# One step of Strassen's scheme in the two output projections of a decoder trunk

## The chip, the cores and the metric

The kernel runs on one core of a Trainium2 chip, as one launch. The metric is the device time of the launch in microseconds (us). The kernel before takes 1911.1 us (median of 3 runs, 1909.24 to 1915.82).

## The reference

The input x has 1024 tokens of width 1024. Two layers follow one another, each with a residual sum, and a shared key and value projection lies between them:

```python
x = x + gated_deltanet_mixer(rms_norm(x, a_norm), ...)   # layer A
k_band, v_band = shared_kv(x, kv_norm, w_kv, k_gain)
x = x + swa_sink_mixer(rms_norm(x, b_norm), ...)         # layer B
# both mixers end in the same way, o is (1024 tokens, 2048):
return o.reshape(B, T, 2048).astype(h.dtype) @ w_out     # w_out (2048, 1024)
```

In layer A, o is the output of a gated delta rule in 8 heads of width 256, normed and multiplied by silu(z). In layer B it is that of a windowed attention with 32 heads of 64, again times silu(z). All is float32. The change touches only the two products `o @ w_out` and the sums with the residual that follow.

## The kernel before, in words

Every large product is made in three matmuls: each factor is cut into a high and a low part (`hi`, `lo`), and hi·hi, hi·lo and lo·hi are accumulated in PSUM. The gated outputs are written to DRAM as transposed rows, `ogT` in layer A and `og2` in layer B (`og` in the rows), 16 blocks of 128 channels by 1024 tokens.

`weight` (L122) makes one weight tile of 128x1024: a DMA of 512 KB on SP's queue into one of two `wraw` buffers, the high part on POOL (L134; weights with a gain are multiplied on POOL, L136, and get theirs on ACT), the low part on DVE (L138). Of the first two tiles after `wcount` is set to 0 or 1 the low part is made on POOL. `take` hands out the next tile and starts as many as `depth` says: two ahead in A, one in B.

`og_load` (L853) loads a quarter of 512 tokens (4 of the 16 blocks) in two DMAs of 512 KB on ACT's queue, casts each half (L862, ACT) and subtracts (L863, DVE).

`out_proj` (L865) is called once per layer. It goes over two halves of the tokens, two column halves `cp` of 512, four quarters `k4` of the channels, two column blocks `b` of 256. For each (k4, b) it takes a weight tile [4, 256], and for 4 token blocks c and 4 channel blocks kk issues three matmuls of 256 moving columns: 2 x 2 x 4 x 2 x 4 x 4 x 3 = 1536 matmuls a projection, 32 weight tiles. Both column halves of one token half share the loaded og; the second half's is loaded during cp = 1. The residual rows `xo` (four tiles of 512 KB for each half, L882) are loaded at (k4, b) = (2, 0). At the end of each cp, four evictions (L893, DVE) add PSUM onto them, and 256 KB stores follow. In A, `finish` then norms the half and transposes it between the matmuls that come next.

Each engine works its instructions in program order, as a scheduler has laid them out ahead of time; an instruction whose input isn't there holds up all behind it on that engine, the DMA issues of that queue too.

Of the kernel before, what the change touches and what calls it, by code (L numbers as in the profile page):

```python
# [64 lines left out]
class Kernel:  # L65
# [56 lines left out]
    def weight(self, src, shape, gain=None):  # L122
# [110 lines left out]
    def layer_a(self):  # L233
        nc, tc, I = self.nc, self.tc, self.I
        with ExitStack() as ctx:
# [72 lines left out]
            for h in range(AH):  # L308
# [6 lines left out]
                if h + 1 == AH:  # L315
                    back += [self.head_z(i, None) for i in late]
                    self.first = self.og_tiles(self.dl0, "kq", "vt")
                    self.og_load(self.ogT, 0, 0, self.first, self.raws)
# [546 lines left out]
    def out_proj(self, og, resid, cur, tiles, raws, px, acc, dst, finish):  # L865
# [3 lines left out]
        for half in range(2):  # L869
            xs, nxt = [], []  # L870
            for cp in range(2):
                cs = slice(cp * 512, cp * 512 + 512)
                ps = [acc.tile([P, 2, 256], F32, name="acc") for _ in range(4)]
                for k4 in range(4):
                    oh, ol = cur[k4]
                    for b in range(2):
                        hi, lo = self.take()
                        if cp == 0 and (k4, b) == (2, 0):
                            self.flush()
                            for c in range(4):  # L880
                                xs.append(px.tile([P, D], F32, name="xo", bufs=4))
                                nc.sync.dma_start(xs[c], resid[half * 4 + c])  # L882
                        for c in range(4):
                            ts = slice(c * P, c * P + P)
                            po = ps[c][:, b, :]
                            for kk in range(4):
                                nc.tensor.matmul(po, oh[:, kk, ts], hi[:, kk, :], start=(k4 + kk + b == 0), stop=False)  # L887
                                nc.tensor.matmul(po, oh[:, kk, ts], lo[:, kk, :], start=False, stop=False)  # L888
                                nc.tensor.matmul(po, ol[:, kk, ts], hi[:, kk, :], start=False, stop=(k4 + kk + b == 7))  # L889
                                if kk % 2:  # L890
                                    self.tick()
                            if (k4, b) == (3, 1):
                                nc.vector.tensor_tensor(out=xs[c][:, cs], in0=ps[c].rearrange("p b c -> p (b c)"),  # L893
                                                        in1=xs[c][:, cs], op=ALU.add)
                                nc.sync.dma_start(dst[half * 4 + c][:, cs], xs[c][:, cs])
                    if half == 0 and cp == 1:
                        nxt.append(tiles(k4))
                        self.og_load(og, 1, k4, nxt[-1], raws)
            cur = nxt
            finish(half, xs)  # L900
# [97 lines left out]
    def layer_b(self, last):  # L998
# [20 lines left out]
        def ahead():  # L1019
            for k4 in range(3):  # L1020
                self.og_load(self.og2, 0, k4, last[k4], raws)
# [4 lines left out]
        self.og_load(self.og2, 0, 3, last[3], raws)  # L1026
# [198 lines left out]
    def run(self):  # L1225
        nc, tc, I = self.nc, self.tc, self.I
        with ExitStack() as ctx:
# [11 lines left out]
            self.wpools, self.wcount = [self.wsp], 0  # L1239
            self.late = (6,)  # L1240
# [5 lines left out]
            with ExitStack() as c1:  # L1246
                hp = pool(c1, "hT")
                self.hT = self.hT_tiles(hp)
                with ExitStack() as c2:
# [23 lines left out]
                    def tiles(k4):  # L1273
                        return self.og_tiles(po, f"oh{k4}", f"ol{k4}") if k4 else self.og_tiles(self.dl0, "kq", "vt")

# [94 lines left out]
```

## Time and profile before

| | us |
|---|---|
| median of 3 runs | 1911.1 |
| profiled execution, its own time | 1906.83 |
| span of the profiled execution | 1905.1 |
| projection A, first to last matmul start | 911.41 to 1098.48 |
| projection B, first to last matmul start | 1716.71 to 1901.01 |
| PE busy in the whole span | 1828.6 (96%) |
| DVE, ACT, POOL busy | 1229.2, 807.5, 536.5 |

Times in the rows are us from the start of the span unless marked ns. PE is TensorE's matmul, PEld its weight load, DVE is VectorE, ACT ScalarE, POOL GpSimd, SP SyncE; a q behind an engine is its queue, which issues DMAs. The mean granted clock is 0.994 of full speed. Everything outside the two projections, some 1530 us, is the same code before and after, except for a few loads at their beginning.

### The profile page before, as it was taken

What the parts mean: (1) busy time and instruction counts of PE and PEld (TensorE: products, weight loads), DVE (VectorE), ACT (ScalarE), POOL (GpSimd) and SP (SyncE); (2) the same over time, 40 slices, a digit from 0 to 9 for tenths busy, and PEclk for the clock granted to TensorE, in tenths of its full rate; (3) what the DMA queues carried; (4) which work ended last, traced back from release to release, by engine and by line L of the source; (5) the groups of instructions that cost most, each with busy time, mean ns of one, the idle gap of its engine ahead of it and who ended that gap; (6) DMA issues with size and microseconds to landing.
All of it is one profiled execution on the core that took longest, in us unless ns stands there. A gap on an engine that the chain in (4) does not pass through costs nothing.

```text
span 1905.1 us, 33635 instructions
## 1 busy us (share of the span) xinstructions
PE 1828.6 (96%) x13186; PEld 1562.9 (82%) x13186; DVE 1229.2 (65%) x2860; ACT 807.5 (42%) x1939; POOL 536.5 (28%) x554
## 2 busy tenths in 40 slices
PE   5999999999999999989999999999999999999999
PEld 4677778787877777767999998888788788879999
DVE  6767776858596776775545266777776776753432
ACT  4545353534435252433112043557756666771100
POOL 2222332323222222221311232333433343322111
PEclk9999999999999999999999999999999999999999
DMA  4511111112011211121655321111201111225542
GB/s 148 122 56 34 56 45 53 37 34 67 23 57 34 65 36 56 45 67 51 238 165 168 111 89 45 40 35 51 67 29 51 56 40 51 73 72 194 190 168 81
DMA packets 150115, 147.62 MB, mean 77 GB/s; under 512 B 7114, under 2 KB 124356, under 8 KB 149956
## 3 DMA queue, kind: packets, MB, share of 16 engines
q1 hardware_dynamic: 139616, 128.30, 21.4%
q10 hardware_dynamic: 10340, 17.16, 2.9%
q8 instruction: 104, 1.70, 0.4%
q14 instruction: 55, 0.45, 0.1%
HBM read 115.00 MB, written 30.44 MB: 76 GB/s over the span
## 4 chain that ended last, share of the span: by engine, by line
PE 36%; DVE 8%; ACT 3%; POOL 3%; issue 2%; DMA 1%; POOLq 0%; SPq 0%; ACTq 0%; DVEq 0%
PE acc L887 6%; PE acc L889 6%; PE acc L888 6%; PE mm L939 3%; PE mm L940 3%; PE mm L941 3%; PE pv L1181 2%; ACT lsb L1150 1%; PE mm L165 1%; PE mm L163 1%; PE mm L161 1%; DVE lsb L1140 1%; DVE wlo L138 1%; POOL lsb L1154 1%; PE tp L1160 1%
## 5 line engine op out<-in xcount | busy, mean ns | idle before, releaser
L161 PE MATMUL mm<-hh,whi 128*128 128x512 f32 (+1 forms) x1040 | 427.1, 411 | 1.8 <-ACT hh L223 1.7
L163 PE MATMUL mm<-hl,whi 128*128 128x512 f32 (+1 forms) x1040 | 417.5, 401 | 1.0 <-DVE hl L224 0.7
L165 PE MATMUL mm<-hh,wlo 128*128 128x512 f32 (+1 forms) x1040 | 414.8, 399 | 0.0
L138 DVE TENSOR_TENSOR wlo<-wraw,whi 128x1024 fp32r<-128x1024 f32 x141 | 178.7, 1268 | 241.0 <-POOL whi L134 216.0
L134 POOL TENSOR_SCALAR whi<-wraw 128x1024 fp32r<-128x1024 f32 x112 | 122.8, 1097 | 476.3 <-PE acc L889 241.4
L161 PEld LDWEIGHTS mm<-hh,whi 128*128 128x128 f32 x1040 | 197.0, 189 | 36.9 <-issue 5.2
L165 PEld LDWEIGHTS mm<-hh,wlo 128*128 128x128 f32 x1040 | 196.7, 189 | 36.5 <-issue 4.2
L163 PEld LDWEIGHTS mm<-hl,whi 128*128 128x128 f32 x1040 | 197.2, 190 | 34.1 <-issue 4.2
L939 PE MATMUL mm<-whi,hh 128*128 128x256 f32 x608 | 180.5, 297 | 0.0
L463 DVE SCALAR_TENSOR_TENSOR acc<-u,cw,acc 128x512 f32<-128x512 f32 x192 | 162.7, 849 | 26.5 <-POOL acc L460 24.3
L940 PE MATMUL mm<-wlo,hh 128*128 128x256 f32 x608 | 172.2, 283 | 0.0
L941 PE MATMUL mm<-whi,hl 128*128 128x256 f32 x608 | 172.2, 283 | 0.0
L887 PE MATMUL acc<-whi,hh 128*128 128x256 f32 x512 | 145.0, 283 | 0.0
L889 PE MATMUL acc<-whi,hl 128*128 128x256 f32 x512 | 144.9, 283 | 0.0
L888 PE MATMUL acc<-wlo,hh 128*128 128x256 f32 x512 | 144.9, 283 | 0.0
L1150 ACT ACTIVATE lsb<-lsb,nm 128x128 f32<-128x128 f32 x256 | 99.8, 392 | 64.1 <-DVE se L1146 54.6
L939 PEld LDWEIGHTS mm<-whi,hh 128*128 128x128 f32 x608 | 116.0, 191 | 11.0 <-issue 10.8
L940 PEld LDWEIGHTS mm<-wlo,hh 128*128 128x128 f32 x608 | 116.3, 191 | 0.2
L941 PEld LDWEIGHTS mm<-whi,hl 128*128 128x128 f32 x608 | 116.0, 191 | 0.0
L460 POOL TENSOR_SCALAR acc<-u,cw 128x512 f32<-128x512 f32 x64 | 63.9, 998 | 183.8 <-ACT u L456 169.6
L1154 POOL TENSOR_TENSOR lsb<-lsb,den 128x512 f32<-128x512 f32 x64 | 68.5, 1070 | 152.6 <-DVE den L1153 51.9
L887 PE MATMUL acc<-whi,oh 128*128 128x256 f32 x384 | 108.5, 283 | 0.0
(351 smaller groups left out, 4287.2 us busy)
## 6 DMA issues: line engine op xcount, KB each, us to landing
wraw<-in_a_w_in SPq DMA_DIRECT2D x48, 512.0 KB, 3.9
wraw<-in_a_w_out SPq DMA_DIRECT2D x32, 512.0 KB, 3.9
wraw<-in_b_w_in SPq DMA_DIRECT2D x32, 512.0 KB, 4.0
wraw<-in_b_w_out SPq DMA_DIRECT2D x32, 512.0 KB, 4.1
og<-zs SPq DMA_DIRECT2D x32, 256.0 KB, 2.0
ogT<-zs SPq DMA_DIRECT2D x28, 256.0 KB, 2.1
btab<-lt SPq DMA_DIRECT2D x1, 4096.0 KB
dm<-gd SPq DMA_DIRECT2D x8, 512.0 KB, 3.7
```

The source lines that it names most:

```text
L134: nc.gpsimd.tensor_scalar(out=hi, in0=raw, scalar1=1.0, scalar2=1.0, op0=ALU.mult, op1=ALU.mult)
L138: (nc.gpsimd if self.wcount < 3 else nc.vector).tensor_tensor(out=lo, in0=raw, in1=self.f32(hi), op=ALU.subtract)
L161: nc.tensor.matmul(ps, hi[:, k, :], hh[:, k, :], start=(k == 0), stop=False)
L163: nc.tensor.matmul(ps, hi[:, k, :], hl[:, k, :], start=False, stop=False)
L165: nc.tensor.matmul(ps, lo[:, k, :], hh[:, k, :], start=False, stop=(k == KT - 1))
L463: nc.vector.scalar_tensor_tensor(out=acc, in0=u[:, t:t + 512], scalar=cw[:, t, blk:blk + 1], in1=acc, op0=ALU.mult, op1=ALU.add)
L887: nc.tensor.matmul(po, oh[:, kk, ts], hi[:, kk, :], start=(k4 + kk + b == 0), stop=False)
L888: nc.tensor.matmul(po, oh[:, kk, ts], lo[:, kk, :], start=False, stop=False)
L889: nc.tensor.matmul(po, ol[:, kk, ts], hi[:, kk, :], start=False, stop=(k4 + kk + b == 7))
L939: nc.tensor.matmul(ps, hh[:, k, ts], hi[:, k % 4, :], start=(k == 0), stop=False)
L940: nc.tensor.matmul(ps, hh[:, k, ts], lo[:, k % 4, :], start=False, stop=False)
L941: nc.tensor.matmul(ps, hl[:, k, ts], hi[:, k % 4, :], start=False, stop=(k == KT - 1))
```

## The change

The tokens, the 2048 channels and the 1024 columns are each cut in two. Instead of eight products of quadrants, seven are made (`PRODUCTS`), each from a sum or difference of og quadrants and of weight quadrants, with signs. Each product has 4 weight tiles j of [2, 512], 4 token blocks c, 2 channel blocks kk and three matmuls of 512 moving columns: 7 x 4 x 4 x 2 x 3 = 672 matmuls a projection.

```python
+    PRODUCTS = (
+        (((1, 0, 0),), ((1, 0, 1), (-1, 1, 1)), ((0, 1, 1), (1, 1, 1))),
+        (((1, 1, 0), (-1, 0, 0)), ((1, 0, 0), (1, 0, 1)), ((1, 1, 1),)),
+        ...
+    )   # terms of og (sign, t, k); terms of w (sign, k, c); sinks (t, q, sign)
...
         nc.sync.dma_start(raw, src)
+        if other is not None:
+            op, src2 = other
+            raw2 = view(self.raw2())
+            nc.sync.dma_start(raw2, src2)
+            nc.gpsimd.tensor_tensor(out=raw, in0=raw, in1=raw2, op=op)
...
-        if gain is None:
+        if other is not None:
+            nc.scalar.copy(out=hi, in_=raw)
+        elif gain is None:
...
+        def quadrant(t, k):
+            if (t, k) not in held:
+                r = held[t, k] = whole(place[t, k])
+                for i in (0, 4):
+                    nc.scalar.dma_start(r[:, i:i + 4, :], ogv[:, 8 * k + i:8 * k + i + 4, 512 * (1 - t):1024 - 512 * t])
...
+            src = [quadrant(t, k) for _, t, k in terms]
+            for j in range(2):
+                ...
+                    nc.vector.tensor_tensor(out=raw, in0=src[0][:, ks, :], in1=src[1][:, ks, :],
...
+                nc.scalar.copy(out=oh[:, js, :], in_=raw)
+                nc.vector.tensor_tensor(out=ol[:, js, :], in0=raw, in1=self.f32(oh[:, js, :]), op=ALU.subtract)
...
+                if (m, j) == (0, 3):
+                    self.flush()
+                    xs = [[px.tile([P, D], F32, name="xo", bufs=8) for _ in range(4)] for _ in range(2)]
+                    ...
+                            nc.sync.dma_start(xs[t][c], resid[(1 - t) * 4 + c])
...
+                        nc.tensor.matmul(ps[c], oh[:, k, ts], hi[:, kk, :], start=(j + kk == 0), stop=False)
...
+                        for t, q, sign in sinks:
+                            x = xs[t][c][:, 512 * q:512 * q + 512]
+                            if sign > 0:
+                                nc.vector.tensor_tensor(out=x, in0=ps[c], in1=x, op=ALU.add)
+                            else:
+                                nc.vector.tensor_tensor(out=x, in0=x, in1=ps[c], op=ALU.subtract)
```

Of a projection's 28 weight tiles 20 are sums or differences: two DMAs of 512 KB, the sum on POOL, the high part on ACT, the low part on DVE. The second raw tile lies in halves of `vv` in A (free once layer A's last gated rows are stored) and in a pool of its own in B. The og factors come as 14 half-products u, two for each product, in a ring of 3 places in A and 4 in B. u = 0 and 1 are loaded by `og_load`. Those after come from whole quadrants of 2.1 MB ("rooms"), each in two DMAs of 1 MB on ACT's queue; A takes layer A's dead inputs `hT` for that (`hh`, `hl` in the rows), B a new pool. Ten of the twelve need 20 DVE sums of 128x1024 in all; each of the 12 needs two casts on ACT and two subtractions on DVE. Each product is evicted onto the residual rows that it belongs to, 12 places in all: 48 evictions of 128x512 a projection. All eight residual tiles (4.2 MB) are loaded in product 0.

The start of projection B on ACT. Before (L862 casts og, L861 loads it, L1089 is silu of the last z, L1183 copies the attention's output):

```order
L1089 ACTIVATE zs_18798<-zs_18798 128x512
L862 CAST hh0_82<-qr_18812 128x1024
L862 CAST hh1_84<-qr_18816 128x1024
L861 DMA qr_18820<-og2_58 128x2x512
L861 DMA qr_18842<-og2_58 128x2x512
L861 DMA qr_18846<-og2_58 128x2x512
L862 CAST hh1_84<-qr_18820 128x1024
L862 CAST hh1_84<-qr_18842 128x1024
L862 CAST hh1_84<-qr_18846 128x1024
```

After (L926 casts og, L908 loads rooms, L141 casts weights; whi_18147 is the high part of the third weight tile, w2, and whi_18191 that of w3):

```order
L908 DMA room1_18092<-og2_58 128x4x512 x2
L908 DMA room0_18095<-og2_58 128x4x512 x2
L926 CAST hh1_84<-oraw_18098 128x1024
L926 CAST hh1_84<-oraw_18102 128x1024
L141 CAST whi_18147<-wraw_18142 128x1024
L908 DMA room2_18175<-og2_58 128x4x512
L926 CAST hh1_84<-oraw_18106 128x1024
L926 CAST hh1_84<-oraw_18110 128x1024
L908 DMA room2_18175<-og2_58 128x4x512
L926 CAST hh0_82<-oraw_18178 128x1024
L926 CAST hh0_82<-oraw_18182 128x1024
L141 CAST whi_18191<-wraw_18186 128x1024
```

The high parts of w2 and w3 stand on ACT now, behind casts of sums of rooms.

The start of projection A on ACT. Before (L841 is the last silu of A):

```order
L841 ACTIVATE acc_9324<-mm_9299 128x512
L862 CAST oh1_9391<-kt_9393 128x1024
L862 CAST oh1_9391<-dm_9397 128x1024
L861 DMA kt_9403<-ogT_57 128x2x512
L861 DMA dm_9407<-ogT_57 128x2x512
L862 CAST oh2_9401<-kt_9403 128x1024
L862 CAST oh2_9401<-dm_9407 128x1024
L861 DMA kt_9413<-ogT_57 128x2x512
L861 DMA dm_9417<-ogT_57 128x2x512
```

After (whi_9426 and whi_9434 belong to w1 and w2):

```order
L850 ACTIVATE acc_9327<-mm_9302 128x512
L908 DMA hh1_84<-ogT_57 128x4x512
L871 CAST oh0_9394<-kt_9398 128x1024
L871 CAST oh0_9394<-dm_9402 128x1024
L908 DMA hl1_85<-ogT_57 128x4x512
L926 CAST oh1_9396<-kt_9410 128x1024
L926 CAST oh1_9396<-dm_9414 128x1024
L908 DMA hl1_85<-ogT_57 128x4x512
L141 CAST whi_9426<-wraw_9422 128x1024
L141 CAST whi_9434<-wraw_9430 128x1024
```

Here also the high parts of w1 and w2 stand behind the casts of u = 1 and u = 2.

The start of projection A on SP. Before (L821 and L846 write the last gated rows of A, L130 loads weights, L882 residual rows):

```order
L821 DMA ogT_57<-zs_8743 128x512
L821 DMA ogT_57<-zs_8981 128x512
L846 DMA ogT_57<-acc_9324 128x512
L130 DMA wraw_9485<-in_a_w_out 128x4x256
L882 DMA xo_9653<-in_x 128x1024
L130 DMA wraw_9539<-in_a_w_out 128x4x256
L882 DMA xo_9655<-in_x 128x1024
L130 DMA wraw_9593<-in_a_w_out 128x4x256
L882 DMA xo_9657<-in_x 128x1024
```

After (L942 loads residual rows, L136 the second raw tile of a sum, L132 the first):

```order
L830 DMA ogT_57<-zs_8981 128x512
L855 DMA ogT_57<-acc_9327 128x512
L942 DMA xo_9542<-in_x 128x1024
L136 DMA vv_9374<-in_a_w_out 128x2x512 x2
L942 DMA xo_9543<-in_x 128x1024
L136 DMA vv_9374<-in_a_w_out 128x2x512 x2
L942 DMA xo_9544<-in_x 128x1024
L132 DMA wraw_9462<-in_a_w_out 128x2x512
L132 DMA wraw_9502<-in_a_w_out 128x2x512
L942 DMA xo_9545<-in_x 128x1024
L136 DMA vv_9374<-in_a_w_out 128x2x512
```

The second raw tiles of w1 and w2 (`vv`) stand behind the last write of gated rows; the first raw tiles were loaded earlier.

## Rows read from the trace of the kernel before

**Rows 1.** Timeline of PE: first and last matmul of each projection; start, length (us).

```profile
911.41 0.36 PE L887 MATMUL acc<-whi,kq 128*128 128x256 f32 x1
...
1098.48 0.28 PE L889 MATMUL acc<-whi,ol 128*128 128x256 f32 x1
...
1716.71 0.39 PE L887 MATMUL acc<-whi,hh 128*128 128x256 f32 x1
...
1901.01 0.28 PE L889 MATMUL acc<-whi,hl 128*128 128x256 f32 x1
```

**Rows 2.** Waits of PE from 905 to 1100 us; none from 1700 to 1905.

```profile
PE acc L888 <- POOL wlo L138: 1.2, 1, 1.2
```

**Rows 3.** Busy time by windows (us, count), granted clock, DMA share, GB/s.

```profile
930.00:1000.00 70.00, 70.00 (x593) 70.00 (x592) 27.57 (x25) 8.10 (x8) 14.60 (x13) 1.00 0.55 176
1750.00:1800.00 50.00, 50.00 (x419) 50.00 (x419) 20.47 (x18) 5.99 (x6) 9.44 (x9) 1.00 0.48 156
```

**Rows 4.** Timeline of PE: matmuls of 512 columns before projection A and in layer B.

```profile
903.23 0.39 PE L161 MATMUL mm<-hh,whi 128*128 128x512 f32 x1
...
905.95 0.39 PE L161 MATMUL mm<-hh,whi 128*128 128x512 f32 x1
...
1670.81 0.39 PE L163 MATMUL mm<-hl,whi 128*128 128x512 f32 x1
...
1671.74 0.39 PE L165 MATMUL mm<-hh,wlo 128*128 128x512 f32 x1
```

**Rows 5.** Single operations by line: count, duration min/median/max in ns, first, last start.

```profile
L138 DVE TENSOR_TENSOR wlo<-wraw,whi x141: 1180/1225/2776, 55.8 to 1890.9; 128x1024 fp32r<-128x1024 f32 x141
...
L138 POOL TENSOR_TENSOR wlo<-wraw,whi x7: 2342/2399/3304, 13.1 to 1730.5; 128x1024 fp32r<-128x1024 f32 x7
...
L134 POOL TENSOR_SCALAR whi<-wraw x112: 1040/1047/2137, 10.2 to 1889.9; 128x1024 fp32r<-128x1024 f32 x112
...
L136 POOL TENSOR_TENSOR wraw<-wraw,gcolb x36: 1892/1897/2933, 1081.8 to 1634.8; 128x1024 f32<-128x1024 f32 x36
...
L893 DVE TENSOR_TENSOR xo<-acc,xo x32: 679/691/694, 955.2 to 1901.3; 128x512 f32<-128x512 f32 x32
...
L862 ACT CAST hh<-qr x8: 1031/1044/1051, 1706.4 to 1726.9; 128x1024 fp32r<-128x1024 f32 x8
...
L863 DVE TENSOR_TENSOR hl<-qr,hh x8: 1212/1226/1909, 1707.5 to 1728.3; 128x1024 fp32r<-128x1024 f32 x8
```

**Rows 6.** Timeline of POOL and DVE beside each other in projection A.

```profile
914.32 2.06 DVE L863 TENSOR_TENSOR ol<-kt,oh 128x1024 fp32r<-128x1024 f32 x1
916.30 3.38 DVE L863 TENSOR_TENSOR ol<-dm,oh 128x1024 fp32r<-128x1024 f32 x1
...
913.28 2.03 POOL L134 TENSOR_SCALAR whi<-wraw 128x1024 fp32r<-128x1024 f32 x1 [1.76 <-DVE acc L845]
915.39 3.21 POOL L138 TENSOR_TENSOR wlo<-wraw,whi 128x1024 fp32r<-128x1024 f32 x1
...
958.74 0.69 DVE L893 TENSOR_TENSOR xo<-acc,xo 128x512 f32<-128x512 f32 x1 [0.75 <-DMA wraw<-in_a_w_out]
...
958.78 1.05 POOL L134 TENSOR_SCALAR whi<-wraw 128x1024 fp32r<-128x1024 f32 x1 [4.72 <-PE acc L889]
```

**Rows 7.** Busy time by windows with DMA at its highest, start of projection A.

```profile
916.00:920.00 4.00, 2.77 (x24) 2.57 (x23) 3.68 (x2) 0.00 (x0) 4.00 (x2) 1.00 1.00 370
```

**Rows 8.** Timeline of ACT (one cast) and of SP's queue (last writes).

```profile
932.44 1.05 ACT L862 CAST oh<-kt 128x1024 fp32r<-128x1024 f32 x1 [4.95 <-DMA kt<-ogT]
...
913.29 0.32 SPq L846 DMA_DIRECT2D ogT<-acc  x1
...
1713.05 5.82 SPq L1092 DMA_DIRECT2D og<-zs  x3
```

**Rows 9.** Timeline of PE after a long idle time, start of the program.

```profile
19.23 0.93 PE L216 MATMUL tr<-cst,kq 128*128 128x128 f32 x2 [11.59 <-DVE kq L209]
...
22.26 0.41 PE L165 MATMUL mm<-hh,wlo 128*128 128x256 f32 x1
```

More of the change, by code (lines that the diff above doesn't have):

```diff
@@ L1 @@
+import itertools
 from contextlib import ExitStack
@@ L120, in rsqrt, with weight @@
         return y
-    def weight(self, src, shape, gain=None):
+    def weight(self, src, shape, gain=None, other=None):
         nc = self.nc
@@ L863, in og_load @@
             nc.vector.tensor_tensor(out=ol[:, js, :], in0=raw, in1=self.f32(oh[:, js, :]), op=ALU.subtract)
-    def out_proj(self, og, resid, cur, tiles, raws, px, acc, dst, finish):
-        nc = self.nc
[L869 to L882, printed above, removed]
-                        for c in range(4):
[L884 to L900, printed above, removed]
@@ L1019, in ahead @@
         def ahead():
-            for k4 in range(3):
-                self.og_load(self.og2, 0, k4, last[k4], raws)
+            for k4 in range(2):
+                self.og_load(self.og2, 1, k4, last[k4], raws)
                 yield 0.0
@@ L1025, in layer_b @@
         self.flush()
-        self.og_load(self.og2, 0, 3, last[3], raws)
     @staticmethod
@@ L1239, in run @@
             self.wpools, self.wcount = [self.wsp], 0
+            self.raw2 = raw2 = lambda: self.wraw.tile([P, 1024], F32, name="wraw")
             self.late = (6,)
@@ L1271, in finish @@
                             self.later((15, 10)[half] + (2, .8)[half] * j, f)
[L1273 to L1280 removed]
+                    ring = [self.first] + [self.og_tiles(po, f"oh{i}", f"ol{i}") for i in range(2)]
+                    room = [self.hT[0][0], self.hT[1][0], self.hT[1][1]]
+                    spare = itertools.cycle(self.vv[:, n:n + 4, :].rearrange("p n c -> p (n c)") for n in (0, 4))
+                    self.raw2 = lambda: next(spare)
+                    self.out_proj(self.ogT, xv, ring, 1, self.raws, lambda i: self.f32(room[i]), px, acc, x1d, finish)
+                    self.raw2 = raw2
                     wk = [self.take(False), self.take(False)]
@@ L1303, in run @@
                     px = pool(c2, "px2", 2)
-                    self.out_proj(self.og2, x1d, last, lambda k4: last[k4],
-                                  lambda j: px.tile([P, 2, 512], F32, name="oraw"), px, pool(c2, "acc2", 6, space=PSUM), ov,
-                                  lambda half, xs: None)
+                    wraw2 = pool(c2, "wraw2", 2)
+                    self.raw2 = lambda: wraw2.tile([P, 1024], F32, name="wraw2")
+                    room = pool(c2, "room")
+                    self.out_proj(self.og2, x1d, last, 2, lambda j: px.tile([P, 2, 512], F32, name="oraw"),
+                                  lambda i: room.tile([P, KT, 512], F32, name=f"room{i}"), px,
+                                  pool(c2, "acc2", 6, space=PSUM), ov, lambda half, xs: None)
     def weights(self):
@@ L1325, in weights @@
                     yield col(self.win, b, None)
-        for _ in range(2):
-            for c in (0, 2):
-                for k in range(4):
-                    for b in range(2):
-                        yield four(rows("a_w_out"), k, c + b, None)
+        yield from self.product_weights(rows("a_w_out"))
         wkv = I["w_kv"].rearrange("(k p) c -> p k c", p=P)
@@ L1340, in weights @@
                 yield col(bin_, 16 + 2 * hg + j, self.gcolb[:, 8:16])
-        for _ in range(2):
-            for c in (0, 2):
-                for k in range(4):
-                    for b in range(2):
-                        yield four(rows("b_w_out"), k, c + b, None)
+        yield from self.product_weights(rows("b_w_out"))
     def dump(self, name, ap):
```

56 lines of the change are left out of this document (50 added, 6 removed), and 5 rows, old and new, of the table PRODUCTS.

## The prediction

> **What bounds the kernel now.** I read the page's first part for the busy shares, then the timeline of PE for the two projections, then what PE waits for in them, then windows inside them. Projection A runs from 911.41 to 1098.48 us, 187.1 us, and B from 1716.71 to 1901.01, 184.3 us [rows 1]. In all that time PE waits once, 1.2 us, for the low part of a weight that POOL makes [rows 2]. Windows from the middle show PE busy to 100%, DVE at 39 to 41%, POOL at 19 to 21%, DMA at about half its share [rows 3]. So PE alone bounds both, and a cheaper product shortens the kernel until another engine's work comes last. The windows give the price of one matmul of 256 columns: 70 us for 593 is 0.1180 in A, 50 for 419 is 0.1193 in B. 1536 of them make 181.3 in A; with the wait, 4.6 us remain, which I give to the transposes of the first normed half. In B it is 183.3 of 184.3.
>
> **Matmuls.** A projection has 672 matmuls of 512 columns after the change. Just before projection A twelve such matmuls take 2.72 us, 0.2267 each; inside layer B four take 0.93, 0.2325 each [rows 4]. A: 672 x 0.2267 = 152.3, and with the 4.6 of transposes, which stay, 156.9: 30.2 less. B: 672 x 0.2325 = 156.2: 28.1 less. Together 58.3 us if nothing waits. A weight tile lasts 24 matmuls, 5.44 us in A and 5.58 in B. What comes after the last matmul (one eviction, one store) stays. Everything else in the sum eats of the 58.3.
>
> **Start of A.** The second weight tile, w1, is due 5.44 us after the first matmul, at 916.9. It is a sum whose second part can't be loaded before the last gated rows, issued at 913.29 [rows 8], have left the memory; I put that between 915.5 and 917. DMA is at its ceiling at that time already before, 370 GB/s from 916 to 920 [rows 7], and now ACT's queue carries rooms beside SP's residual rows and raw tiles. If the two queues share evenly, w1's 0.5 MB behind one residual tile costs 2.1 MB, 5.7 us: it lands at about 922.7, and w2's 2.8 us later. POOL then adds w1, waits for w2's part and adds that, and only then subtracts w1's low part: a sum on POOL costs 1.90, a low part 2.40 to 3.30 [rows 5]. 922.7 + 2.8 + 1.9 + 2.4 = 929.8, a wait of 12 or 13 us. The high parts of w1 and w2 on ACT stand behind casts of rooms that need some 3 MB, which ends at about the same time. The low bound has the raw tiles first: 918.3 + 1.4 + 2 x 1.2 + 2.4, 7.6 us; the high one 15, where the rooms hold ACT. I take 12. Before, the same start had the one wait of 1.2 us.
>
> **Start of B.** w0 and w1 are ready; w2 is due 11.2 us after the first matmul. Its high part waits on ACT behind two casts of u = 2, and those behind two sums on DVE whose sources are room 1 and the first half of room 0. Rooms can't be loaded before the last og2 rows are written, issued to about 1718.9 [rows 8], which is 2 us after PE's start. Queued ahead on ACT's queue stand three DMAs of 1.05 MB; on SP two raw tiles (1.05 MB) and then 4.2 MB of residual rows. Shared evenly at 370 GB/s [rows 7], 6.3 MB need 17 us. Behind the landing come two sums of 1.2, two casts and the high part of 1.05, and POOL's low part of 2.4, 6.8 us with what overlaps [rows 5]: ready at 2 + 17 + 6.8 = 25.8, a wait of 15 us. w3 stands behind the first half of room 2 in the same way: 5.25 MB on ACT and as much on SP, 28 us, then 7 of sums, casts and low part, ready at 37.5, due 5.6 after w2, at 31.4: 6 or 7 us more. Together 22. Bounds: without the residual rows, 4.2 MB for w2 and little more for w3, 13 us; with the residual rows wholly ahead, 8.4 MB, 28 us. That loads on ACT's queue are slow beside residual rows is seen before: a cast at 932.44 had waited 4.95 us for 0.5 MB [rows 8]. I keep 22, between them, nearer to the high end, because of that row. The Trainium skill, "DMA: Bandwidth & Descriptors", section "Queues, rings and completion order", says that each DMA engine goes round the queues that have work, a packet at a time; residual rows come in pieces of 4 KB and rooms in pieces of 2 KB, so by it the rooms would get a third and the wait would be near 28. No run here shows the share.
>
> **The clock.** After an idle time of 11.59 us PE's matmuls were 0.41 us long still at 22.26, 3.4 us after it began again, against 0.28 at the full 2.4 GHz [rows 1, 9]: half of that lost, 1.7 us. Three waits are that long or near it: 1.7 in A, 3.4 in B. Bounds 0 and twice this.
>
> **In the steady state.** DVE gets per projection 27 low parts of weights x 1.225, 28 of og x 1.226, 20 sums x 1.226 (its price the subtraction's, of one shape) and 48 evictions x 0.691 [rows 5]: 33.1 + 34.3 + 24.5 + 33.2 = 125.1 us. POOL gets 20 sums x 1.897 and 8 high parts x 1.047, 46.3 us. Both fit beside 152 to 156 us of PE; ACT has 48 casts of 1.05, 50 us. But DVE and POOL stop each other: with DVE's subtractions of two SBUF tiles beside it, POOL's high part took 2.03 instead of 1.05 and its low part 3.21, and DVE's subtractions took 2.06 and 3.38 [rows 6]. An eviction from PSUM kept its 0.69 beside POOL's 1.05 [rows 6]. The Trainium skill, "SBUF — State Buffer", section "Who interferes with whom", has this as an exclusive lock on a shared port, which an operation of DVE with one SBUF input doesn't touch; the trace agrees, as those rows show. So 125.1 - 33.2 + 46.3 = 138.2 us of work must stand one behind the other, which 152 still holds; if POOL never falls beside an eviction it is 171.4. The loss is thus between 0 and 171.4 - 152.3 = 19 in A, 0 and 15 in B. A low part late by a few us is what PE would wait for. I take the quarter next to the low end, 5 in A and 4 in B, because 138 fits and two of 6 PSUM buffers stay free at the change from one product to the next. DMA in steady state: a weight tile and its second part are 1.05 MB in 5.5 us, 191 GB/s, and rooms and rows beside it stay under the 370.
>
> **The sum.** A: 156.9 + 12 + 1.7 + 5 = 175.6, 11.5 less than 187.1. B: 156.2 + 22 + 3.4 + 4 = 185.6, 1.3 more than 184.3. Net 10.2 less: 1906.83 becomes 1896.6 for a profiled execution. The median of the runs was 4.3 above the profiled one, so 1901.
>
> **Rivals.**
> 1. The starts are mostly hidden. For it: the rooms in A reuse memory that is free early, and the low bounds above add to 7.6 and 13. With half of these, 10 us in all, and a steady state without loss, 58.3 - 10 - 1.7 = 46.6 less: 1864. Against it: DMA is full at that very time in the kernel before [rows 7].
> 2. Slower: the lock between DVE and POOL decides. Each POOL sum then holds up a subtraction, so that DVE and POOL take 171.4 us a projection; this decides from the point where fewer than 19 of POOL's 46.3 us (171.4 less PE's 152.3) fall beside evictions. A: 171.4 + 4.6 + 12 + 1.7 = 189.7, 2.6 more; B: 171.4 + 22 + 3.4 = 196.8, 12.5 more; 1926. For it: rows 6 show nearly every overlap paid in full. Against: evictions make up 33 us at the end of every product, just where POOL has a raw buffer to fill, and before, the same two engines worked through a whole projection without a wait of PE [rows 2].
> 3. Hardly any gain by PE: 512 columns in a projection cost twice the 0.1180 and 0.1193 of 256. A 158.6, B 160.3: 10.4 more than forecast, 1911, no change. Against: rows 4 have the cheaper pitch at full PE twice, with the same kinds of operands.
>
> **How the numbers follow.** Forecast 0.52, rival 1 0.15, rival 2 0.18, rival 3 0.15. About 0.3%, 5.7 us, is what a measurement of this kernel can tell from no change. With all terms at their low ends (7.6, 13, no clock, no lock) the sum gives 1873, at their high ends (15, 28, 10.2, 34) 1940; the forecast's own range goes half-way to each, 1887 to 1920, and lies to two thirds under 1905.4. With rival 1 and a little of rival 3 faster gets 0.55. Same, 1905.4 to 1916.8: a quarter of the forecast and most of rival 3, 0.23. Slower: rival 2 and a rest, 0.22. The range for 8 in 10 reaches towards rival 1 and rival 2, 1868 to 1922.
>
> **What would show it.** In the trace after: 24 matmuls of one weight tile in 5.44 and 5.58 us; a wait of PE of about 12 us near 917, released by POOL's low part of w1; waits of 15 and 7 us near 1728 and 1742, released by the weights' high or low part behind casts and rooms; granted clock under 1 behind each; DMA at 370 GB/s in those stretches; DVE at some 125 us busy or more in each projection, and small waits of PE for low parts. Wrong it would be if PE's waits in the middle of a projection sum to over 15 us (rival 2), if the starts wait under 10 us together (rival 1), or if the matmuls themselves stand 0.236 us apart (rival 3).

## The result and the profile after

The changed kernel takes 1939.99 us (median of 4 runs, 1933.61 to 1943.23) against 1910.17 for the kernel before in the same runs. The ratio is 1.0154, with a 95% interval of 1.0131 to 1.0177: 30 us slower, where 10 us faster was forecast, and outside the range of 1868 to 1922. The profiled execution took 1933.61 us, its span is 1931.9, 26.8 more than before.

The timeline of PE with the first and last matmul of each projection in the changed kernel (start, length in us) answers to [rows 1]:

```profile
909.50 0.48 PE L948 MATMUL acc<-whi,kq 128*128 128x512 f32 x1
...
1108.40 0.40 PE L950 MATMUL acc<-whi,ol 128*128 128x512 f32 x1
...
1726.94 0.50 PE L948 MATMUL acc<-whi,hh 128*128 128x512 f32 x1
...
1927.54 0.39 PE L950 MATMUL acc<-whi,hl 128*128 128x512 f32 x1
```

A takes 198.9 us instead of 187.1, B 200.6 instead of 184.3, and between them nothing changed (618.5 against 618.2). So the loss lies inside the projections, 11.8 and 16.3 us; A began 1.9 earlier. The waits of PE (line and releaser, us in total, times, longest), A first and then B, answer to [rows 2]:

```profile
PE acc L948 <- ACT whi L141: 18.6, 3, 17.0
PE tr L225 <- DVE xo L218: 6.9, 5, 4.1
PE acc L949 <- DVE wlo L147: 3.9, 2, 2.1
PE acc L949 <- POOL wlo L147: 2.7, 1, 2.7
PE acc L948 <- DVE xo L958: 1.7, 1, 1.7
...
PE acc L948 <- ACT whi L141: 19.8, 6, 9.9
PE acc L949 <- DVE wlo L147: 7.1, 6, 2.6
PE acc L949 <- POOL wlo L147: 7.1, 2, 5.3
```

Before, PE waited once in A, 1.2 us, and not at all in B; now it waits 34 us in each. Three groups can be told apart by place. At the start of A PE waits 17.0 and 2.7 us at w1, at that of B 9.9 and 1.7 at w2, 5.8 and 5.3 at w3. The transposes of the first normed half in A wait 6.6 us (four of the five waits in the second line; the fifth lies behind A). The rest, 8 us in A and 11 in B, are waits of 0.2 to 2.6 us for single weight tiles and evictions.

Adding up the 672 steps from one matmul to the next gives the whole account. A: 152.3 for matmuls at 0.2267, 1.6 for steps slightly longer (0.229 in the mean), 34.5 of waits, 6.3 for matmuls at half clock, 4.5 for the transposes. B: 152.7, 34.0 of waits, 14.1 at half clock. The half clock is seen in the granted clock of windows (third column from the right), here three late in B:

```profile
1838.00:1841.00 3.00, 1.96 (x9) 1.30 (x7) 0.00 (x0) 0.97 (x2) 2.95 (x2) 1.00 0.04 14
1841.00:1844.00 3.00, 2.12 (x7) 1.52 (x8) 2.90 (x3) 1.02 (x2) 0.09 (x1) 0.90 0.75 217
1844.00:1847.00 3.00, 3.00 (x9) 2.33 (x8) 2.14 (x4) 0.00 (x0) 0.00 (x0) 0.53 0.78 255
```

PE had waited 1.2 and 0.8 us there, and its matmuls then came 0.427 instead of 0.227 us apart for 3.4 us. There are five such stretches in B and two in A, 11.0 and 3.7 us of the half clock given above; the rest is single slow steps behind waits.

**Start of B.** The timelines of SP, POOL and ACT (queue issues have a q; idle time before, in brackets):

```profile
1730.08 0.95 SPq L136 DMA_DIRECT2D wraw<-in_b_w_out  x2
1731.12 0.45 SPq L942 DMA_DIRECT2D xo<-x1d  x1
1740.67 0.37 SPq L136 DMA_DIRECT2D wraw<-in_b_w_out  x1
1741.09 8.15 SPq L942 DMA_DIRECT2D xo<-x1d  x7
...
1727.53 11.02 ACTq L908 DMA_DIRECT2D room<-og  x3
1744.79 2.18 ACT L926 CAST hh<-oraw 128x1024 fp32r<-128x1024 f32 x2 [16.30 <-DVE oraw L924]
...
1746.88 1.04 ACT L141 CAST whi<-wraw 128x1024 fp32r<-128x1024 f32 x1
1751.55 2.18 ACT L926 CAST hh<-oraw 128x1024 fp32r<-128x1024 f32 x2 [3.63 <-DVE oraw L924]
...
1760.50 2.23 ACT L926 CAST hh<-oraw 128x1024 fp32r<-128x1024 f32 x2 [6.77 <-DVE oraw L924]
1762.64 1.04 ACT L141 CAST whi<-wraw 128x1024 fp32r<-128x1024 f32 x1
...
1738.30 4.63 POOL L137 TENSOR_TENSOR wraw<-wraw,wraw 128x1024 f32<-128x1024 f32 x2 [17.01 <-DMA wraw<-in_b_w_out]
1748.00 2.44 POOL L147 TENSOR_TENSOR wlo<-wraw,whi 128x1024 fp32r<-128x1024 f32 x1 [5.06 <-ACT whi L141]
1764.18 2.34 POOL L137 TENSOR_TENSOR wraw<-wraw,wraw 128x1024 f32<-128x1024 f32 x1 [13.74 <-DMA wraw<-in_b_w_out]
1766.47 3.33 POOL L147 TENSOR_TENSOR wlo<-wraw,whi 128x1024 fp32r<-128x1024 f32 x1
```

The second raw tiles, asked for at 1730, landed at 1738. POOL's sums of w2 and w3 took 4.63, so w2's was done near 1740.6, but its high part stood on ACT until 1746.88 behind two casts of og, just as in the order shown ahead of the prediction. The low part came at 1750.4 from POOL. w3's sum was done near 1742.9; its high part came at 1763.7 behind four more casts, which waited for rooms, and its low part at 1769.8 behind POOL's sum of w4. Of the residual rows one tile went out at 1731 and the other seven from 1741 on, because SP's queue stood until 1740.6 at the second part of w4, whose buffer POOL's first sum had to free. From 1730 to 1756 the DMA share was 1.03, at 390 GB/s. This start cost 22.7 us of waits; 22 were forecast.

**Start of A.** The second raw tiles went out at 921.5, not 917, because the last gated rows before them were written out at 915.1 and landed only 6.4 us later; the tiles needed 7 us more to land, and POOL then took 4.64 us for two sums. Counted from the first matmul, that write went out after 5.6 us; in the kernel before it was 1.9.

```profile
915.12 0.32 SPq L855 DMA_DIRECT2D ogT<-acc  x1
...
921.51 1.46 SPq L136 DMA_DIRECT2D vv<-in_a_w_out  x2
...
928.82 4.64 POOL L137 TENSOR_TENSOR wraw<-wraw,vv 128x1024 f32<-128x1024 f32 x2 [20.23 <-DMA vv<-in_a_w_out]
933.42 2.35 POOL L147 TENSOR_TENSOR wlo<-wraw,whi 128x1024 fp32r<-128x1024 f32 x1
```

**Transposes in A.** The norm of the first half now shares ACT with weights: two of its four squares stood behind a high part that waited for POOL, and eight evictions instead of four stand before it on DVE (L956, 1074.84 to 1079.71); the matmuls of the transposes stand in PE's order at a fixed place.

```profile
1076.80 1.06 ACT L208 ACTIVATE sq<-xo 128x1024 bf16<-128x1024 f32 x1
...
1081.61 1.05 ACT L141 CAST whi<-wraw 128x1024 fp32r<-128x1024 f32 x1 [3.66 <-POOL wraw L137]
1082.56 1.05 ACT L208 ACTIVATE sq<-xo 128x1024 bf16<-128x1024 f32 x1
```

### The profile page after: what moved, and what is told of

The parts are those of the page before. It is cut to its first block, busy times and chain, and to the rows that moved or that the text cites. A ratio compares the mean times of both kernels' runs of the same rounds, so it can differ in the third digit from the quotient of the medians.

```text
span 1931.9 us, 30401 instructions
## 1 busy us (share of the span) xinstructions
PE 1786.2 (92%) x11458; PEld 1452.0 (75%) x11458; DVE 1355.5 (70%) x2980; ACT 872.0 (45%) x2003; POOL 584.8 (30%) x546
## 3 DMA queue, kind: packets, MB, share of 16 engines
q1 hardware_dynamic: 131936, 145.08, 23.6%
## 5 line engine op out<-in xcount | busy, mean ns | idle before, releaser
L147 DVE TENSOR_TENSOR wlo<-wraw,whi 128x1024 fp32r<-128x1024 f32 x133 | 185.0, 1392 | 150.7 <-ACT whi L141 73.9
L472 DVE SCALAR_TENSOR_TENSOR acc<-u,cw,acc 128x512 f32<-128x512 f32 x192 | 162.9, 851 | 26.3 <-POOL acc L469 24.1
L143 POOL TENSOR_SCALAR whi<-wraw 128x1024 fp32r<-128x1024 f32 x64 | 73.0, 1140 | 241.7 <-PE mm L172 142.6
L948 PE MATMUL acc<-whi,hh 128*128 128x512 f32 x224 | 92.2, 412 | 19.9 <-ACT whi L141 19.8
L949 PE MATMUL acc<-wlo,hh 128*128 128x512 f32 x224 | 91.9, 410 | 14.2 <-DVE wlo L147 7.1
L141 ACT CAST whi<-wraw 128x1024 fp32r<-128x1024 f32 x40 | 41.9, 1047 | 128.7 <-POOL wraw L137 128.7
L145 POOL TENSOR_TENSOR wraw<-wraw,gcolb 128x1024 f32<-128x1024 f32 x36 | 72.6, 2017 | 88.0 <-DMA wraw<-in_b_w_in 57.5
```

What stands on the lines that cost most here:

```text
L147: (nc.gpsimd if self.wcount < 3 else nc.vector).tensor_tensor(out=lo, in0=raw, in1=self.f32(hi), op=ALU.subtract)
L472: nc.vector.scalar_tensor_tensor(out=acc, in0=u[:, t:t + 512], scalar=cw[:, t, blk:blk + 1], in1=acc, op0=ALU.mult, op1=ALU.add)
L948: nc.tensor.matmul(ps[c], oh[:, k, ts], hi[:, kk, :], start=(j + kk == 0), stop=False)
L949: nc.tensor.matmul(ps[c], oh[:, k, ts], lo[:, kk, :], start=False, stop=False)
```

## The experiments

Lengths are from the first to the last matmul start of a projection in the profiled execution; "waits" adds the idle times of PE inside it, "half clock" what the steps over 0.27 us lasted beyond 0.2267 (some 3 us of it are slower first steps behind each wait). Where an edit leaves a projection as it is, A lies at 198.9 to 200.5 in three profiles, B at 198.3 to 200.6 in three and at 194.5 in b_only; each length comes from one profile, so a difference inside these spreads shows nothing.

| kernel | ratio to before (95%) | A, waits, half clock | B, waits, half clock |
|---|---|---|---|
| changed | 1.0154 (1.0131 to 1.0177) | 198.9, 34.5, 6.3 | 200.6, 34.0, 14.1 |
| a_only | 1.0060 (1.0033 to 1.0087) | 199.8, 33.0, 8.6 | 184.3 (as before) |
| b_only | 1.0055 (1.0036 to 1.0073) | 187.1 (as before) | 194.5, 30.1, 12.0 |
| fill | 1.0168 (1.0140 to 1.0196) | 204.9, 19.7, 8.9 | 195.8, 12.8, 9.9 |
| turns | 1.0190 (1.0164 to 1.0216) | 200.6, 34.7, 9.8 | 200.1, 33.0, 14.7 |
| xo_half | 1.0140 (1.0121 to 1.0159) | 199.1, 31.8, 9.2 | 197.2, 31.0, 13.8 |
| b_raw | 1.0136 (1.0111 to 1.0162) | 200.5, 32.2, 9.7 | 196.1, 34.1, 9.5 |
| late_u | 1.0157 (1.0139 to 1.0174) | 198.4, 30.6, 9.7 | 205.0, 32.9, 19.6 |
| a_raw2 | 1.0126 (1.0107 to 1.0145) | 197.6, 29.1, 10.6 | 198.3, 31.7, 14.2 |
| lo_dve | 1.0139 (1.0121 to 1.0158) | 198.1, 29.6, 10.4 | 198.0, 31.9, 13.5 |
| early | 1.0095 (1.0065 to 1.0125) | 191.6, 20.2, 13.3 | 197.9, 34.0, 11.5 |
| mix1 | 1.0027 (1.0017 to 1.0038) | 191.4, 20.6, 13.0 | 188.8, 29.8, 6.6 |
| mix2 | 1.0042 (1.0025 to 1.0058) | 191.1, 19.5, 13.4 | 189.0, 24.1, 12.5 |
| mix2_b | 1.0006 (0.9992 to 1.0019) | 187.1 (as before) | 185.5, 23.7, 9.3 |
| mix4_b | 0.9975 (0.9963 to 0.9987) | 187.1 (as before) | 182.5, 17.1, 13.0 |
| mix4_b8 | 0.9969 (0.9955 to 0.9984) | 187.1 (as before) | 179.5, 17.5, 9.7 |

**a_only and b_only: one projection alone.** The edit keeps the old `out_proj` beside the new one, with the old list of weights for the other projection.

> Only projection A in seven products, projection B as before. From the two traces A grew from 187.1 to 198.9 us and began 1.9 us earlier, B grew from 184.3 to 200.6. Theory (each projection loses by itself: late parts of sums at its start, later the release of raw buffers): A near 199 us, B near 184.5, the whole about 10 us (0.5%) slower than before. Rival (the loss of B is partly inherited, for example from stores of A or from a clock that is lower for the rest): the whole 3 us or less, or 20 or more, slower.

> Only projection B in seven products, projection A as before. Theory: A near 187, B near 200, the whole about 16 us (0.85%) slower than before. Rival (losses depend on each other): under 8 or over 24 us slower.

Each loses by itself, 11 us in A and 10 in B (0.60% and 0.55%); together they make 1.15%, a little under the changed kernel's interval. A met its number. B alone lost less than expected: 194.5 us. A's length is the same with and without a changed B, and B's differs by 6 us at most with and without a changed A; so a disturbance of 8 us or more is out, and a few us of it in B stay open.

**fill: does PE's idling lower the clock?**

```
+        fill = {(0, 1): 80} if ready == 1 else {(0, 2): 44, (0, 3): 46}
...
+                for _ in range(fill.get((m, j), 0)):
+                    nc.tensor.matmul(idle, oh[:, 0, :P], oh[:, 0, :], start=True, stop=True)
```

> The changed kernel with 80 more matmuls of 512 columns ahead of the second weight tile of A, and 44 and 46 ahead of the third and fourth of B, on data that lie ready; their sums are thrown away. They fill about the time in which PE waits there. Theory (the wait ends by data, and the slow clock behind it comes from PE's idling): the waits end at the same times as before, the granted clock stays near 1.00 behind them, and the three stretches of matmuls 0.43 us apart go: about 6 us less than the changed kernel. Rival (the clock is lowered by something else in the stretch, such as the load on DMA): clock and time as in the changed kernel, or longer by what the fill runs over.

The timeline of PE in fill, around w1 in A:

```profile
924.65 14.67 PE L947 MATMUL acc<-kq 128*128 128x512 f32 x64
939.15 0.39 PE L952 MATMUL acc<-whi,kq 128*128 128x512 f32 x1
941.87 0.50 PE L953 MATMUL acc<-wlo,kq 128*128 128x512 f32 x1 [2.33 <-POOL wlo L147]
942.21 0.40 PE L954 MATMUL acc<-whi,vt 128*128 128x512 f32 x1
```

w1's low part came 26.5 us after the first matmul, as in the changed kernel (26.3), and the matmuls behind it ran 0.23 us apart at once, with a granted clock of 1.00 from 939 to 945, where the changed kernel had 0.50 to 0.52 up to 939. The DMA share was 0.88 there. So at w1 it was PE's own idling that lowered the clock, and not the load on DMA. In B the other two stretches that were to go stayed: the fill ended 2.0 us before w2's low part and 1.8 us before w3's, and behind each of these waits the matmuls ran at half clock again, with a granted clock of 0.76 from 1765 to 1772 and from 1785 to 1792.

```profile
1767.27 0.79 PE L953 MATMUL acc<-wlo,hh 128*128 128x512 f32 x1 [2.02 <-POOL wlo L147]
1767.86 0.63 PE L954 MATMUL acc<-whi,hl 128*128 128x512 f32 x1
```

Half clock in B fell from 14.1 to 9.9; B's 195.8 us lie inside the spread of the unfilled B. A became longer (204.9 us): its later short waits and stretches at half clock grew, for a cause that stays open. The 6 us forecast were not won; the total is unchanged.

**turns: is the transposes' place at fault?** In this kernel the key and value product begins before the last transposes of the first half, which come out too late for it.

```
-                            self.later((15, 10)[half] + (2, .8)[half] * j, f)
+                            self.later((24, 10)[half] + (2, .8)[half] * j, f)
```

> The changed kernel with the transposes of the first normed half of A put 9 turns (6 us) later between the matmuls of the seventh product. Theory (PE waits 6.6 us for the norm, whose chain starts behind 8 evictions instead of 4, and then runs at half clock for 4 us): about 8 us less in A, 190 to 191 us. Rival (the norm comes last in any case, and what is moved is waited for at the end of A): A within 2 us of 198.9.

The waits of 6.6 us went, and a wait of 5.7 us for the transposes' low parts stood at the end of A instead. A took 200.6 us although four of the eight groups of transposes ran only after its end: the rival's number. At the later place the norm was done in time; late was now the cast of the transposes on ACT (1106.82), behind a weight's cast (1105.86) that had waited for POOL. So the wait moved on.

**xo_half, b_raw, late_u, a_raw2, lo_dve: one suspected cause each.**

> The changed kernel with the residual rows loaded in two parts: the right column halves (2.1 MB) in product 0, where they are needed first, the left ones in product 1. Theory (at the start of B two queues share about 390 GB/s, so the parts of w2, w3 and w4 and the rooms land late in proportion to the bytes asked for): the fourth tile's wait in B, 11.1 us with POOL's low part, falls by 4 to 6 us, the third's hardly, since its parts were issued ahead of the rows; A's wait at w1 by at most 1 us. Whole: 4 to 8 us less than the changed kernel. Rival (the waits at the start of B come from the order on ACT alone): no change within 2 us.

```
+                if (m, j) in ((0, 3), (1, 3)):
+                    qs = slice(512 * (1 - m), 512 * (1 - m) + 512)
...
+                            nc.sync.dma_start(xs[t][c][:, qs], resid[(1 - t) * 4 + c][:, qs])
```

w3's waits fell from 11.1 to 8.4 us, w2's stayed (11.7). Direction right, size half.

> The changed kernel with a third buffer for raw weight tiles in projection B. Theory (late in B a raw tile is asked for only when the low part of the tile two before is made; landing 4.2, sum 2.4, cast 1.0 and low part 1.2 us leave hardly 2 us of slack, so any delay on SP or DVE ends in a wait of PE): the waits after 1800 us, 11 us in all with their stretches at half clock of 10 us, fall to a third; B near 188 instead of 200. Rival (DVE and POOL hold each other up there): waits stay, B within 3 us of 200.

```
+                    more, turn = pool(c2, "more"), itertools.cycle((1, 0, 0))
+                    self.raw1 = lambda: (more if next(turn) else self.wraw).tile([P, 1024], F32, name="wraw")
```

The waits behind 1800 us fell from 11 to 6.5 (they are 8.0 to 10.9 in the four profiles with this B unchanged), but in the start they grew (16.2 at w2, 10.5 at w3). That points to the chain of raw buffers as one cause of the late waits. B's 196.1 us are not the 188 forecast and lie inside the spread of the unchanged B.

> The changed kernel with the sums and casts of the second product's og (u = 2, and 3 in B) placed after the fourth weight tile of product 0 instead of ahead of the product. Theory (w2's and w3's high parts wait on ACT behind casts of rooms that have not landed): in B w2 comes 5 us earlier and w3 without a wait, but w4, whose raw tile is asked for behind the residual rows, becomes the wait: B 5 to 8 us shorter. In A, where ACT waited for POOL, nothing changes within 2 us. Rival (the rooms' landing decides, in whatever order): B within 2 us of 200.

```
-        for u in range(ready, len(ring)):
+        for u in range(ready, 2):
             load(u)
...
                 if (m, j) == (0, 3):
+                    for u in range(2, len(ring)):
+                        load(u)
```

w2 waited 6.6 instead of 11.6 and w3 6.1 instead of 11.1, and seven waits of 0.7 to 2.3 us appeared in the second and third product. The theory holds for w2, whose wait is 5 us shorter. w3 did not come without a wait: 4.5 of its 6.1 us are for POOL's low part. B as a whole got longer, 205.0 us, not 5 to 8 shorter.

> The changed kernel with the second raw tiles of A in the dead key buffer instead of the value buffer, so that their first loads need not wait for the last write of gated rows. Theory (the wait of 19.8 us at w1 is that write's late landing, 6.4 us behind 4.2 MB of rooms, then a load of 7 us): the two loads go out before 912, land near 918, and w1's wait falls to about 8 us, with A near 187. Rival (full DMA decides: the load lands as late among the rooms): the wait stays above 16 us.

```
-                    spare = itertools.cycle(self.vv[:, n:n + 4, :].rearrange("p n c -> p (n c)") for n in (0, 4))
+                    spare = itertools.cycle(self.kn[:, n:n + 4, :].rearrange("p n c -> p (n c)") for n in (0, 4))
```

The loads went out at 917.9, 6.9 us after the first matmul, behind the same write in SP's order, and w1's sum began at 926.9. Its wait fell from 19.8 to 16.7: the rival's number. The memory that was waited for was worth 3 us. The loads did not go out before 912 as the theory has it, so what an earlier load is worth is shown not here but by early.

> The changed kernel with the low parts of the first weight tiles of both projections (w1 in A, w2 and w3 in B) made on DVE instead of POOL. Theory (POOL's low part of 2.4 to 3.3 us stands behind POOL's sum of the next tile, so PE waits for it once more after the high part): the waits for POOL's low parts, 2.7 in A and 1.7 and 5.3 in B, fall to about 1.2 each: 6 us less than the changed kernel. Rival (DVE is held up by POOL's sums at that time, and the next tile is late anyway): under 2 us.

```
-                    self.wpools, self.wcount, self.depth = [self.wsp, wx, self.wsp], 1, 2
+                    self.wpools, self.wcount, self.depth = [self.wsp, wx, self.wsp], 4, 2
...
-                self.wpools, self.wcount, self.depth = [self.wsp], 0, 1
+                self.wpools, self.wcount, self.depth = [self.wsp], 4, 1
```

The waits for low parts fell from 2.7 to 1.5 in A and, at w3, from 5.3 to 0.7; at w2 it rose from 1.7 to 2.9, and a later tile waited 3.2. Of these five kernels none can be told from the changed one by its total; they are read by their stages.

**early: the first missing tile asked for sooner.**

```
+                    self.fetch()
```

The line stands in `run` ahead of both projections, before `self.raw2` is changed.

> The changed kernel with one more weight tile asked for ahead of each projection (w1 in A, w2 in B), its second part in the ordinary raw buffers, so that both parts are loaded and summed before DMA is full. Theory (at the starts the raw parts' late landing is what PE waits for): A's wait moves from w1 (19.8 us) to w2 and is 8 to 11 us, B's wait for w2 (11.6) goes nearly, and w3's stays at 11 or grows by up to 6: 12 to 20 us less than the changed kernel. Rival (DMA is short of the bytes of the first two products together, so that what is gained at one tile is lost at the next): the waits of each start sum to within 4 us of 20 and 23.

In A the 19.8 us at w1 became 3.9 there, 2.2 and 1.3 at the next tiles and 5.1 in the second product: A 7.3 us shorter. In B w2 waited 2.5 and w3 21.1, together about what w2 and w3 waited in the changed kernel. So A won, though less than the theory has it: the waits at the start sum to 12.5 us and are spread over four tiles, and half clock rose from 6.3 to 13.3. For B the rival's number holds.

**mix1: those edits together** (without late_u, with four places for second raw tiles in A).

> All edits that shortened a projection, together: residual rows in two parts, a third raw buffer in B, four places for second raw tiles in A, the first low parts on DVE, and one more weight tile asked for ahead of each projection. If their gains add up: A 199 - 12, B 200 - 20, near 1908 us, level with the kernel before. If DMA at the starts is the floor: A 195, B 192, 1923 or more.

It is 0.27% slower than before. The early tile removed w2's wait in B, and w3 got all of it. The timelines of POOL and ACT show why, in mix1:

```profile
1736.62 2.40 POOL L137 TENSOR_TENSOR wraw<-wraw,wraw 128x1024 f32<-128x1024 f32 x1 [0.32 <-DMA wraw<-in_b_w_out]
...
1747.03 2.18 ACT L926 CAST hh<-oraw 128x1024 fp32r<-128x1024 f32 x2 [17.03 <-DVE oraw L924]
1752.32 2.18 ACT L926 CAST hh<-oraw 128x1024 fp32r<-128x1024 f32 x2 [3.11 <-DMA xo<-x1d]
1759.23 2.23 ACT L926 CAST hh<-oraw 128x1024 fp32r<-128x1024 f32 x2 [4.73 <-DMA room<-og]
1761.37 1.99 ACT L141 CAST whi<-wraw 128x1024 fp32r<-128x1024 f32 x2
```

w3's sum was ready at 1739.0; its high part came 22 us later, behind six casts of og that weren't needed before it.

**mix2 and mix2_b: that order mended.**

```
-        for u in range(ready, len(ring)):
+        for u in range(ready, 2):
...
                 if (m, j) == (0, 3):
+                    for u in range(2, len(ring) + 1):
+                        load(u)
...
-                if j % 2 and 2 * m + j // 2 + len(ring) < 14:
+                if j % 2 and m + j > 1 and 2 * m + j // 2 + len(ring) < 14:
```

> The kernel with all the edits together (mix1) and the og of the second product made after the fourth weight tile, in the order in which its parts are needed. There w3's sum was ready at 1739 us, and its high part stood on ACT until 1761 behind casts of rooms. Theory (the order on ACT, not the bytes, made that wait of 23 us): w3 comes without a wait, what is late next is the second product's og, by 3 to 8 us; B near 172 instead of 188.8, A within 4 us of 191, the whole 1900 to 1904, under the kernel before. Rival (DMA is short of the bytes of the first two products whatever the order): waits of 18 to 23 us stay spread over the next tiles; B 184 or more, the whole 1912 or more.

> The same, in B only; A as before the change. A 187 us again. Theory: B near 172, the whole 12 us under the kernel before, about 1899. Rival: B 184 or more, no gain.

w3's wait of 22.7 us went, and B was as long as before (189.0; 185.5 in mix2_b): the rival. Windows of mix2_b show DMA at its ceiling from 1720 to 1760 (328 GB/s in the first 5 us, 386 to 388 behind them), and DVE at 100% from 1740 to 1770:

```profile
1725.00:1730.00 5.00, 5.00 (x24) 4.14 (x23) 0.00 (x0) 0.18 (x1) 2.39 (x1) 1.00 1.05 388
...
1740.00:1745.00 5.00, 1.92 (x4) 0.99 (x5) 5.00 (x6) 2.09 (x2) 0.03 (x1) 0.75 1.05 388
...
1755.00:1760.00 5.00, 0.00 (x0) 0.00 (x0) 5.00 (x4) 1.42 (x2) 2.77 (x1) 0.61 1.06 387
1760.00:1770.00 10.00, 3.48 (x9) 2.76 (x10) 10.00 (x11) 2.76 (x3) 0.00 (x0) 0.51 0.61 213
```

These 40 us make 15 MB: rooms, residual rows and weights of the first products.

**mix4_b and mix4_b8: the order on DVE, and more PSUM.**

```
-                    for u in range(2, len(ring) + 1):
+                    for u in range(2, max(4, len(ring))):
...
-                if j % 2 and m + j > 1 and 2 * m + j // 2 + len(ring) < 14:
-                    load(2 * m + j // 2 + len(ring))
+                if j % 2 and m and 2 * m + j // 2 + 2 < 14:
+                    load(2 * m + j // 2 + 2)
...
-                                  pool(c2, "acc2", 6, space=PSUM), ov, lambda half, xs: None)
+                                  pool(c2, "acc2", 8, space=PSUM), ov, lambda half, xs: None)
```

> The kernel of mix2_b (seven products in B only, with all the edits) with each half-product of og from the third on made one half-product later. There the seventh weight tile's high part was done at 1754.7 us and its low part stood on DVE until 1765 behind the sums and subtractions of og for the third product: a wait of 12.7 us. Theory (what is left of the loss at the start is the order on DVE): that wait goes or falls to 3 us, the waits of B sum to 12 instead of 24, B near 172, the whole near 1898, 0.6% under the kernel before. Rival (DMA at its ceiling for 40 us and DVE full behind it are the floor): the wait moves on, B stays above 182, no gain.

> mix4_b with 8 instead of 6 PSUM buffers in B. Theory: a product then starts without any eviction of the one before being done, so the waits for evictions (1.6 us in mix2_b) go, and late evictions cost nothing: 1 to 3 us less than mix4_b. Rival: evictions were never what PE waited for to any amount: same time.

The 12.7 us wait went; waits of 2.8, 1.2, 3.1 and 2.0 took a part of its place. B came to 182.5, the rival's bound, and the gain is half of the 0.6% forecast. With 8 buffers the waits for evictions (4.4 us in mix4_b) went and B came to 179.5, but the waits still sum to 17 us. Both kernels are faster than the kernel before, by 0.25% and 0.31%; from each other they can't be told by their totals. What PE still waits for in B of mix4_b8:

```profile
PE acc L990 <- DVE wlo L147: 14.8, 5, 6.5
PE acc L989 <- ACT hh L963: 2.4, 1, 2.4
```

The theory's 12 us of waits came out as 17, and B 7.5 to 10.5 us over the 172 expected: DVE's low parts are now the last, and 10 to 13 us of half clock are left.

## Why the prediction was wrong

- **Matmuls.** Right: 0.2267 us in A and 0.2273 in B (0.2325 forecast). The shorter list alone is worth what was said, or 3 us more in B.
- **Start of B.** Right in sum (22.7 for 22), but not in its parts, and that they cancel is luck: w2 waited 11.6 us, not 15, and w3 11.1, not 7. The mechanism, a weight's high part behind og casts on ACT, is seen in b_raw, early and mix1, and late_u shortened w2's wait by taking the casts away. What failed is SP's order: the forecast has all residual rows beside w2's rooms, but seven of the eight tiles went out only from 1741 on and stood beside w3's. mix2 shows that DMA's ceiling and then DVE stand right behind the order on ACT.
- **Start of A.** Mis-sized: 19.8 us for 12, over the bound of 15. The step that failed is the issue of w1's second part "between 915.5 and 917", measured at 921.5. Counted from the first matmul, the write ahead of it went out 3.7 us later than before (5.6 for 1.9). It took 6.4 us to land where 917 leaves 3.7, with DMA at 402 to 405 GB/s from 909 to 915. The load itself took 7.1 us instead of 5.7. These make up the 7.8 us; POOL's part, 7.1 us from the landing to the low part, was as forecast.
- **The clock.** Price about right, number wrong, and the largest miss in B: 14.1 us for 3.4, in A 6.3 for 1.7, outside the bound of twice the forecast in both. A stretch costs 1.5 to 3.3 us (forecast 1.7); but waits of 0.8 to 2.6 us brought it too, so there were five in B, not two, and the many waits add 3 us of slow first steps in each projection.
- **Steady state.** Mis-sized: 8 us for 5 in A and 11 for 4 in B, inside the bounds (19 and 15). The reason given, that DVE and POOL stop each other, is seen on DVE and seldom on POOL, whose sums lasted 2.40 us in the median and 2.34 at least. Of DVE's 143 operations of 128x1024 on two SBUF tiles in the two projections 20 lasted 1.8 to 3.4 us instead of 1.22, each beside work of POOL: 28 us more in all. The four longest waits for DVE's low parts, 2.1 and 1.8 us in A and 1.8 and 2.6 in B, ended with a part that lasted 2.3 to 3.1 us beside a sum on POOL (the first is shown below). The time by which these four were longer, 5.3 us, is a quarter of the 19 us of waits. b_raw points to the chain of raw buffers (low part, load, sum) for others, and mix2_b to DVE's order.
- **Transposes.** Left out: "which stay" was the failing step. Their work stays (4.5 us), but the norm behind twice as many evictions and a weight's cast made PE wait 6.6 us. This is read from the trace; no run shows it, since turns, which moved their place, traded one wait for another.

The first of the four low parts named under the steady state, and the sum on POOL beside it:

```profile
965.25 2.57 DVE L147 TENSOR_TENSOR wlo<-wraw,whi 128x1024 fp32r<-128x1024 f32 x1 [4.35 <-ACT whi L141]
...
964.38 2.36 POOL L137 TENSOR_TENSOR wraw<-wraw,vv 128x1024 f32<-128x1024 f32 x1 [0.24 <-DMA vv<-in_a_w_out]
```

The sum: A 7.8 (start) + 4.6 (clock) + 3 (steady) + 6.6 (transposes) + 1.6 (pitch) = 23.6 over the forecast of 175.6, measured 23.3. B 0.7 + 10.7 + 7.3 - 3.5 = 15.2 over 185.6, measured 15.0. Rival 2 came nearest (1926), but by its own sign, over 15 us of waits in the middle of a projection, it did not happen: these are 14.7 us in A with the transposes and 11.3 in B. The sum with all terms at their high ends gives 1940, the time measured; that is luck, since the clock and the start of A lie above their bounds, the transposes had none, and the start of B and the steady state lie inside. None of the prediction's three signs of being wrong came.

The duration of a POOL sum is where a row was read too freely:

```profile
L137 POOL TENSOR_TENSOR wraw<-wraw,vv x19: 2337/2407/3373, 928.8 to 1081.5; 128x1024 f32<-128x1024 f32 x19
L137 POOL TENSOR_TENSOR wraw<-wraw,wraw x18: 2337/2392/3487, 1738.3 to 1912.2; 128x1024 f32<-128x1024 f32 x18
```

The prediction took the 1.897 of a product with a broadcast gain from [rows 5], and in the low bound of A's start even 1.2; the low part on POOL, 2.40 with two whole inputs, was the nearer row. The Trainium skill ("GPSIMD Engine Reference", section "Elementwise — side-by-side cycle accounting") gives 4497 ns for such a sum of 2048 elements, half of which for 1024 is an estimate of 2.25; the trace's 2.34 agrees.

## What to carry to other kernels

A shorter list on the bounding engine is worth only what its suppliers can follow: here each projection asked DMA for 8 MB more of weights, and DVE, ACT and POOL for sums and casts, at a start for which almost none of it had been made ahead. Count waits and not only their length, for each of a microsecond or two may cost another two of slow clock behind it. In an order of instructions fixed ahead, put what is due first first: in mix1 a cast whose input was ready stood 22 us behind others not yet due, and when that was mended the next engine had the same fault.

## What was not expected of the hardware

- The granted clock fell to half behind two waits of 1.2 and 0.8 us (at 1842), yet stayed at 1.00 behind waits of 0.5 and 2.1 us (at 968). In fill a wait of 2.3 us in A left it at 1.00, and one of 2.0 us in B did not. What PE did before them was not told apart by these runs.
- Residual rows and rooms did not share DMA evenly, as the forecast took it. From 1750 to 1758 us SP's queue (q1) moved residual rows alone, in pieces of 4 KB, and ACT's (q10) rooms in pieces of 2 KB: 2.06 and 1.13 MB, so the rooms had 141 of 399 GB/s, 35%. The lines show packets, MB and the share of the 16 DMA engines' time in that window.

```profile
q1 hardware_dynamic: 566, 2.06, 65.4%
q10 hardware_dynamic: 567, 1.13, 37.2%
```

This is the third that the prediction worked out from the Trainium skill ("DMA: Bandwidth & Descriptors", section "Queues, rings and completion order"), and the trace agrees with it. It did not bring the 28 us, because seven of the eight residual tiles were held back until 1741.
